# A list scheduler reckons later landings for its transfers, and the order is searched anew under them

## The chip, the cores and the metric

The kernel runs on one core of one Trainium2 chip. The metric is the device time of one launch in microseconds (us), as the median of several runs. The core has TensorE (PE in the profile) for matrix products, VectorE (DVE), ScalarE (ACT), GpSimd (POOL) and SyncE (SP). SP and POOL start transfers (DMAs) between device memory and the on-chip memory here. Each engine works through its own instructions in the order in which they were issued; between engines, semaphores make one wait for another.

## The reference

Two layers (`DEPTH = 2`) act on `x` of 512 tokens and 1024 channels. Both branches of a layer start from one projection of the normalised input.

```python
def hybrid_layer(...):
    h = rmsnorm(x, norm_g)
    proj = h @ w_in
    aq, ak, av, az, bqk, bv, bi, bf, bo, bz, ga, gb = jnp.split(proj, idx, axis=-1)
    ...
    oa = diff_attention(q, k, v, lam)                  # 8 heads: two softmax maps each, subtracted
    oa = rmsnorm(oa, attn_norm_g) * (1.0 - lam_init) * silu(az)
    ya = oa @ w_out_a
    qk = jax.nn.silu(causal_conv(bqk, conv_w, conv_b))
    hb = mlstm_chunkwise(mq, mk, mv, i_pre, f_pre)     # 8 heads: num / max(|den|, exp(-m))
    hb = sigmoid(bo) * rmsnorm(hb, mlstm_norm_g) * silu(bz)
    yb = hb @ w_out_b
    u = sigmoid(ga) * ya + sigmoid(gb) * yb
    return x + u @ w_o
```

All of it is float32.

## The kernel before

**Precision and pieces.** A float32 operand is split into a high part, rounded to the format float32r that PE multiplies, and a low part, the rest. A product then takes three matmuls: high by high, high by low, low by high. The names end in h and l: `hh`, `hl` for the normalised input, `wh`, `wl` for weights. Weights come in pieces of 128x1024 (512 KB). The projections are named as in the reference (`az`, `bqk`, `bo`, `bz`, `ga`, `gb`), `woa` and `wob` are the two output projections of the branches, `wo` the last one. A piece is the slice of weights for 128 output channels: `bo6` is the seventh of `bo`, and `wr92`, `wh92`, `wl92` are the raw, high and low tiles of the 93rd piece in the order of work. The products `bv` and `wo` are computed by a scheme of seven products (`P1` to `P7`) from sums of weight pieces (`wws`, `wwt`) and sums of inputs.

**How a piece becomes ready.** Normally `load` has SP transfer the piece into `wr`, of which there are two buffers, and `prep` has ACT cast it to `wh` and DVE subtract to get `wl`. For the names in `TUNE["dlo"]`, `dload` goes another way: POOL transfers the piece to `dh`, ACT writes its rounded negative to `dl`, and POOL transfers the piece a second time with an addition into `dl`. So `dl` is the low part without DVE or a buffer of `wr`. The sums for the seven products are made by adding transfers of POOL as well, where DVE doesn't make them.

**Heads.** Each of the eight mLSTM heads loads its decay terms in four transfers (`dd`, SP), makes scores with PE (`ms`, from `mq`, `mql` and `mk`), multiplies them with `dd`, splits them (`sdh`, `sdl`) and then sums for numerator (`num`) and denominator (`den`). `den` is a product with a matrix of ones; `msp_a` and `msp_b` are such sums for the norms of the two branches. The summand is either split over 128 rows into two parts (`hi_lo`: `msh`, `msl`, two matmuls of 128x512), or, for the heads in `foldA`, `foldM` and `foldD`, its two halves of 64 rows are added first, and the high and low parts of the sum share one tile `fo` (`fold`, one matmul):

```python
b = t2(f"fb_{name}")[L]
yield b
hl = t2(f"fo_{name}", F32R)
V.tensor_tensor(a[L], a[L], b, ALU.add)
A.copy(hl[L], a[L])
V.tensor_tensor(hl[H], a[L], hl[L].bitcast(F32), ALU.subtract)
```

**What sets the order.** The program first records every operation, with its engine, its cost by a formula and the operations it depends on, in the order of the string `TUNE["order"]` (pieces) and of due times (`attn`, `ml`, `ap`, `m0`, `mp` ...), which say after how much matmul work a head's steps are recorded. `schedule` (L293 to L443) then plays a simulation of the engines: again and again it takes the engine that can start first and picks on it the ready operation with the smallest key. Keys are nominal PE time plus a number for each kind of tile, `TUNE["bias"]`. SP takes its operations in recorded order. A transfer occupies one common road for its bytes over a rate (`rate`: 360 bytes per ns for weights, 175 for `rows` and copies, 150 for adding ones), and is reckoned landed 2000 ns after the road has it (L427). POOL spends 1000 ns on issuing one. `issue` (L462 to L469) emits all operations in the order that came out, so that nearly every row of the profile has the line L469, and table loads of ACT L468. What is on the chip is thus a fixed order per engine; the simulation's times are not.

Of the kernel before, what the change touches and what calls it, by code (L numbers as in the profile page):

```python
# [35 lines left out]

TUNE = {
    "order": (
# [4 lines left out]
    ),  # L43
    "qkt": 5,
    "gct": 18,
    "gls": 0,
    "glf": 1,
    "attn": (0, 5, 5, 9, 11, 13, 16, 16, 19, 27),
    "a0": 24,
    "ap": 18,  # L50
    "a4": 9,
    "ml": (0, 9, 16, 18, 18, 32),
    "ahead": 3,
    "lc": 4,
    "slack": 3188.5,
    "margin": 0.0,
    "pemargin": 16.8,
    "wait": 431.4,
    "swpen": 141896579.9,
    "smargin": 63.5,  # L60
    "pwait": 0.0,
    "wdiff": 7238.9,
    "wsp": 4,
    "kact": (0, 1, 2),
    "qsq": (1, 3),
    "foldA": (2, 3, 5, 6, 7),
    "foldM": (0, 1, 2, 3, 4, 5),
    "foldD": (0, 1, 2, 4, 5, 7),
    "warm": 18,
    "start": 'x0 ct ng w0 x1 w1 x2 x3',  # L70
    "prods": 'P1 P5 P2 P6 P3 P7 P4',
    "acl": 6,
    "gateA": 8,
    "gateM": 6,
    "actp": (0, 2),
    "m0": 220,
    "mp": 13,
    "m4": 9,
    "slots": 24,
    "hfd": 1,  # L80
    "tset": (0, 18),
    "silu": (),
    "pmask": 0,
    "dlo": ('az0', 'bo6', 'woa4', 'wob5'),
    "dla": 7,
    "groups": (),
    "vkeep": (('av', 0), ('av', 1), ('bv', 0), ('bv', 1)),
    "qspill": {},
    "vl": {('av', 0): 50, ('av', 1): 140, ('bv', 0): 228, ('bv', 1): 272},
    "tdve": {'bv': ('T2',), 'wo': ('T1', 'T2', 'T3')},  # L90
# [32 lines left out]
class Recorder:  # L123
# [169 lines left out]
    def schedule(self):  # L293
# [44 lines left out]
        end = [0.0] * n  # L338
        dma = 0.0
# [20 lines left out]
        while len(order) < n:  # L360
# [18 lines left out]
            s, e = best  # L379
# [18 lines left out]
            i = pick[1]  # L398
# [1519 lines left out]
```

## Time and profile before

| | before |
|---|---|
| runs | 1342.16, 1343.46, 1343.55 us, median 1343.46 |
| profiled execution | 1341.84 us, of which the span is 1340.1 us |
| granted clock of TensorE | 0.999 |
| instructions in the span | PE 6152 matmuls, DVE 1906, ACT 1880, POOL 68 |
| transferred | 158.62 MB, mean 118 GB/s |

The span runs from the first to the last instruction of the profiled execution; the 1.74 us around it are launch and end. The views used below are: the first rows of the page (busy time of each engine), the table of waits (which instruction stood idle and what ended it: time in total, number, longest), the windows (a stretch's start and end, its length, the busy time and number of instructions of PE, weight loads, DVE, ACT and POOL, the granted clock, the DMA share and GB/s), the chain that ended last (start, length, what), the instructions of one tile (shortest, median and longest duration in ns, first and last start) and the transfers (KB each, median us from issue to landing). "A <- B" in a wait means that A waited for B; in an instruction's name it means output from inputs.

### The profile page before, as it was taken

The page shows a single profiled execution, that of the slowest core. Times are in us where ns is not written, and L with a number is a line of the kernel's source. Part 1 is how long each engine was busy: PE and PEld are TensorE (multiplying, and loading weights), DVE is VectorE, ACT ScalarE, POOL GpSimd, SP SyncE. Part 2 cuts the span into 40 slices and gives each one's busy share as a digit, 9 for nine tenths or more (in the row PEclk, how much of TensorE's full clock was granted, in tenths as well). Part 3 has the DMA queues.
Part 4 walks back from the last instruction along what each step waited for, and adds up shares of the span by engine and source line. Part 5 has one row for each costly group of instructions (what it writes and reads, how often), then busy time and mean ns, then how long its engine had stood idle before and what let it go on. Part 6 is the DMA issues. An engine that isn't in the chain of part 4 may idle for free.

```text
span 1340.1 us, 17612 instructions
## 1 busy us (share of the span) xinstructions
PE 1320.6 (99%) x6152; PEld 1084.7 (81%) x6152; DVE 1065.2 (79%) x1906; ACT 925.0 (69%) x1880; POOL 55.2 (4%) x68
## 2 busy tenths in 40 slices
PE   9999999999999999999999999999999999999998
PEld 7888888888788787788788888888887887878886
DVE  7899889896588878755888988889866888787476
ACT  6878789794467787743667787888935578778242
POOL 1000000000010000001100000000001000000000
PEclk9999999999999999999999999999999999999999
DMA  6222222235364444346842232232455545353555
GB/s 218 71 65 82 76 79 81 94 94 162 119 157 118 131 117 122 99 139 156 263 125 70 65 95 64 79 99 75 113 136 159 144 119 149 80 144 97 160 152 168
DMA packets 54152, 158.62 MB, mean 118 GB/s; under 512 B 6416, under 2 KB 13200, under 8 KB 54064
## 3 DMA queue, kind: packets, MB, share of 16 engines
q1 hardware_dynamic: 48304, 136.54, 33.2%
q0 software_dynamic: 5760, 20.97, 8.1%
q8 instruction: 48, 0.79, 0.2%
q14 instruction: 40, 0.33, 0.1%
HBM read 153.23 MB, written 4.26 MB: 118 GB/s over the span
## 4 chain that ended last, share of the span: by engine, by line
PE 82%; DVE 6%; ACT 5%; DMA 5%; issue 2%; SPq 0%; DVEq 0%; ACTq 0%; POOLq 0%
PE qk L469 13%; PE av L469 9%; PE az L469 7%; PE ga L469 7%; PE woa L469 7%; PE wob L469 7%; PE gb L469 6%; PE bqk L469 5%; PE bv_P L469 4%; PE wo_P L469 4%; PE bz L469 3%; PE sc L469 3%; DMA wr<-in_wp_dram 3%; PE bo L469 2%; PE num L469 1%
## 5 line engine op out<-in xcount | busy, mean ns | idle before, releaser
L469 ACT CAST wh<-wr 128x1024 fp32r<-128x1024 f32 (+1 forms) x194 | 202.0, 1045 | 130.3 <-PE woa L469 32.7
L469 DVE TENSOR_TENSOR wl<-wr,wh 128x1024 fp32r<-128x1024 f32 (+1 forms) x196 | 233.8, 1197 | 35.4 <-ACT wh L469 34.4
L469 PE MATMUL qk<-wl,hh 128*128 128x512 f32 x256 | 96.1, 399 | 0.3 <-DVE wl L469 0.3
L469 PE MATMUL qk<-wh,hh 128*128 128x512 f32 x256 | 95.1, 397 | 0.6 <-ACT hh L469 0.6
L469 PE MATMUL qk<-wh,hl 128*128 128x512 f32 x256 | 94.8, 395 | 0.1
L469 ACT ACTIVATE p<-sc,mx,rq 128x128 f32<-128x128 f32 (+3 forms) x128 | 78.8, 619 | 9.8 <-DVE mx L469 6.8
L468 ACT ACT_TABLE_LOAD x61 | 78.3, 1283 | 1.0
L469 PE MATMUL woa<-oa,wh 128*128 128x512 f32 x224 | 73.2, 391 | 0.0
L469 PE MATMUL wob<-ob,wh 128*128 128x512 f32 x224 | 70.9, 389 | 0.0
L469 PEld LDWEIGHTS qk<-wl,hh 128*128 128x128 f32 x256 | 48.1, 188 | 10.4 <-DVE wl L469 1.1
L469 ACT CAST ks<-qkt 64x256 fp32r<-64x256 f32 x128 | 47.0, 367 | 13.5 <-DVE qs L469 12.1
L469 PEld LDWEIGHTS qk<-wh,hl 128*128 128x128 f32 x256 | 48.0, 188 | 9.8 <-DVE hl L469 0.4
L469 PEld LDWEIGHTS qk<-wh,hh 128*128 128x128 f32 x256 | 47.6, 188 | 10.0 <-ACT hh L469 0.8
L469 DVE TENSOR_REDUCE mx<-sc 128x2 f32<-128x256 f32 (+1 forms) x64 | 52.4, 818 | 0.7
L469 PE MATMUL ga<-hl,wh 128*128 128x512 f32 x128 | 50.9, 398 | 0.0
L469 PE MATMUL ga<-hh,wl 128*128 128x512 f32 x128 | 50.5, 395 | 0.0
L469 PE MATMUL ga<-hh,wh 128*128 128x512 f32 x128 | 50.3, 393 | 0.0
L469 PE MATMUL bqk<-hh,wh 128*128 128x512 f32 x128 | 50.2, 392 | 0.0
L469 PE MATMUL bqk<-hh,wl 128*128 128x512 f32 x128 | 50.2, 392 | 0.0
L469 PE MATMUL gb<-hh,wh 128*128 128x512 f32 x128 | 50.0, 391 | 0.0
L469 PE MATMUL bqk<-hl,wh 128*128 128x512 f32 x128 | 50.0, 391 | 0.0
L469 PE MATMUL gb<-hl,wh 128*128 128x512 f32 x128 | 49.9, 390 | 0.0
(355 smaller groups left out, 3841.7 us busy)
## 6 DMA issues: line engine op xcount, KB each, us to landing
wr<-in_wp_dram SPq DMA_DIRECT2D x192, 512.0 KB, 3.6
wws_wo<-in_wp_dram POOLq DMA_DIRECT2D x12, 512.0 KB, 7.1
dh<-in_wp_dram POOLq DMA_DIRECT2D x8, 512.0 KB, 3.9
dl<-in_wp_dram POOLq DMA_DIRECT2D x8, 512.0 KB, 7.2
dd<-rows SPq DMA_DIRECT2D x16, 256.0 KB, 4.0
wws_bv<-in_wp_dram POOLq DMA_DIRECT2D x8, 512.0 KB, 9.3
em<-rows SPq DMA_DIRECT2D x16, 256.0 KB, 4.7
dd<-rows SPq DMA_DIRECT2D x16, 192.0 KB, 5.3
```

What stands on the lines that cost most here:

```text
L468: self.tc.keep_in_program_order(self.nc.scalar.preload_act_table_set(self.SET_NAME[o["load"]]))
L469: self.tc.keep_in_program_order(getattr(o["e"], o["fn"])(*o["a"], **o["k"]))
```

## The change

One rule of the scheduler and the table `TUNE` change. A transfer is reckoned landed 3000 ns after the road has it, and 5500 ns if POOL issues it, where both were 2000 ns:

```diff
                 dma = max(dma, go) + size / self.rate(o)
-                end[i] = max(dma, go) + 2000.0
+                end[i] = max(dma, go) + (5500.0 if e == "POOL" else 3000.0)
```

In the table, the order of the pieces, the due times, the scheduler's margins and all biases are others; a line or two of them stand here for the rest:

```diff
-        "woa2 woa0 woa3 woa1 woa4 woa5 woa6 bv.P1 bv.P5 bv.P2 bv.P3 bv.P6 bv.P7 bqk0 bv.P4 bqk1 bo1 bqk6 bz1 bo0 bz0 "
+        "woa7 woa4 woa1 ga5 woa3 woa5 bv.P1 woa0 bv.P5 bv.P2 bv.P3 bv.P6 bv.P7 bqk0 bqk1 bv.P4 bo1 bqk6 bz1 bo0 bz0 bo4 "
...
-    "ml": (0, 9, 16, 18, 18, 32),
+    "ml": (4, 7, 12, 13, 22, 37),
...
-    "qsq": (1, 3),
-    "foldA": (2, 3, 5, 6, 7),
-    "foldM": (0, 1, 2, 3, 4, 5),
-    "foldD": (0, 1, 2, 4, 5, 7),
+    "qsq": (3,),
+    "foldA": (1, 2, 3, 4, 5, 7),
+    "foldM": (0, 1, 2, 3, 4, 5, 6, 7),
+    "foldD": (0, 1, 2, 3, 4, 5, 6, 7),
...
-    "acl": 6,
+    "acl": 7,
-    "actp": (0, 2),
+    "actp": (0, 1, 2, 3),
...
-    "dlo": ('az0', 'bo6', 'woa4', 'wob5'),
-    "dla": 7,
+    "dlo": ('az0', 'az6', 'bo1', 'bo4', 'bo6', 'bo7', 'bqk3', 'bz3', 'bz4', 'ga3', 'gb5', 'woa4', 'wob1', 'wob5'),
+    "dla": 5,
```

`dla` says how many pieces ahead `dload` looks, `acl` how many pieces ahead the sums are begun, `actp` for which token tiles ACT and not DVE scales the second softmax map, `qsq` for which token tiles ACT also sums the squares of q and k, which DVE does for the others. Of the 14 names in `dlo`, 13 are taken in each layer (for `az6` there is no room). The programs differ by this count: matmuls 6152 to 6142, transfers of POOL for `dh` and `dl` 8 to 26 each, transfers of SP 18 fewer, all of them `wr`. Both layers have the same order in themselves.

The order moves most instructions. Three places of layer 0 show how.

The first is SP's queue at the decay terms `dd` and `em` of heads 5 to 7 and the weight loads `wr87` to `wr90`. Before:

```order
L469 DMA wr87_996<-in_wp_dram 128x1024
L469 DMA wr88_1002<-in_wp_dram 128x1024
L469 DMA em0_5_980<-rows_107 128x512
L469 DMA dd0_7_1033<-rows_107 128x512
L469 DMA dd0_7_1033<-rows_107 128x384
L469 DMA dd0_7_1033<-rows_107 128x256
L469 DMA dd0_7_1033<-rows_107 128x128
L469 DMA wr89_1023<-in_wp_dram 128x1024
L469 DMA em0_6_1007<-rows_107 128x512
L469 DMA wr90_1029<-in_wp_dram 128x1024
```

And of the change, the same place:

```order
L469 DMA wr87_996<-in_wp_dram 128x1024
L469 DMA wr88_1002<-in_wp_dram 128x1024
L469 DMA em0_5_956<-rows_107 128x512
L469 DMA dd0_6_961<-rows_107 128x512
L469 DMA dd0_6_961<-rows_107 128x384
L469 DMA dd0_6_961<-rows_107 128x256
L469 DMA dd0_6_961<-rows_107 128x128
L469 DMA wr89_1008<-in_wp_dram 128x1024
L469 DMA em0_6_987<-rows_107 128x512
L469 DMA dd0_7_992<-rows_107 128x512
```

The load `wr89` stood behind the terms of head 7; it now stands behind those of head 6 and ahead of those of head 7. On ACT, its cast stood 8 rows behind that of `wr87`, whose buffer it takes over; now 26 rows.

The second is ACT around that cast and the denominator of head 6 (`dd0_6`, `msh_d0_6`, `fo_d0_6`). Before:

```order
L469 CAST fo_b0_5_992<-ms_b0_5_990 64x512
L469 ACTIVATE tbz0_6_1001<-bz0_6_999 128x512
L469 CAST wh88_1003<-wr88_1002 128x1024
L469 CAST wh89_1024<-wr89_1023 128x1024
L468 ACT_TABLE_LOAD
L469 ACTIVATE ms_b0_5_990<-ms_b0_5_990 128x512
L469 CAST msh_d0_6_1014<-dd0_6_1006 128x512
L469 ACTIVATE ms_b0_5_990<-ms_b0_5_990 128x512
```

And of the change:

```order
L469 CAST wh89_1009<-wr89_1008 128x1024
L469 COPY fb_d0_6_1014<-dd0_6_961 64x512
L469 ACTIVATE dd0_7_992<-dd0_7_992,gcol0_298 128x128
L469 ACTIVATE dd0_7_992<-dd0_7_992,gcol0_298 128x256
L468 ACT_TABLE_LOAD
L469 ACTIVATE ms_b0_5_984<-ms_b0_5_984 128x512
L469 CAST fo_d0_6_1015<-dd0_6_961 64x512
L469 ACTIVATE ms_b0_5_984<-ms_b0_5_984 128x512
```

The two weight casts no longer stand one right behind the other ahead of the table load; `wh88` now stands five rows ahead of `wh89`. Head 6 is folded, and its `fb_d` and `fo_d` take the place of `msh_d`. On PE the two matmuls for `den0_6` stood among those of `bz0_7`; the one that is left stands within the products of `num0_6`. The four `mq` casts of the fourth tile (`mq0_3`) stood in one group right behind `fb_d0_5`; two of them now stand ahead of it.

The third is POOL from the last sums of `bv` on. Before:

```order
L469 DMA wws0_bv_0_701<-in_wp_dram 128x1024
L469 DMA wws0_bv_1_706<-in_wp_dram 128x1024
L469 MEMSET mql00_0_779 64x1024
L469 MEMSET mql10_0_780 64x1024
L469 DMA dh81_887<-in_wp_dram 128x1024
L469 DMA dl81_888<-in_wp_dram 128x1024
L469 MEMSET mql00_1_931 64x1024
L469 MEMSET mql10_1_932 64x1024
```

And of the change:

```order
L469 DMA wws0_bv_0_696<-in_wp_dram 128x1024
L469 DMA wws0_bv_1_701<-in_wp_dram 128x1024
L469 DMA dh67_772<-in_wp_dram 128x1024
L469 MEMSET mql00_0_780 64x1024
L469 MEMSET mql10_0_781 64x1024
L469 DMA dl67_773<-in_wp_dram 128x1024
L469 DMA dh72_805<-in_wp_dram 128x1024
L469 DMA dl72_806<-in_wp_dram 128x1024
L469 DMA dh76_842<-in_wp_dram 128x1024
L469 DMA dl76_843<-in_wp_dram 128x1024
```

Where one pair `dh`, `dl` stood between the sums and the second set of memsets (`bo6`, piece 81), there now stands a row of pairs for pieces 67 (`bo1`), 72, 76 and more. At the start of the program, the first `dh` stood ahead of two memsets of `kl` on POOL and now stands behind them.

More of the change, by code (lines that the diff above doesn't have):

```diff
@@ L38 @@
     "order": (
[4 rows of a table removed]
[4 rows of a table added]
     ),
     "qkt": 5,
-    "gct": 18,
-    "gls": 0,
+    "gct": 17,
+    "gls": 1,
     "glf": 1,
-    "attn": (0, 5, 5, 9, 11, 13, 16, 16, 19, 27),
+    "attn": (0, 4, 6, 10, 10, 13, 14, 16, 19, 26),
     "a0": 24,
     "ap": 18,
-    "a4": 9,
-    "ml": (0, 9, 16, 18, 18, 32),
+    "a4": 18,
+    "ml": (4, 7, 12, 13, 22, 37),
     "ahead": 3,
     "lc": 4,
-    "slack": 3188.5,
+    "slack": 1705.4,
     "margin": 0.0,
-    "pemargin": 16.8,
-    "wait": 431.4,
+    "pemargin": 59.5,
+    "wait": 229.8,
     "swpen": 141896579.9,
-    "smargin": 63.5,
-    "pwait": 0.0,
-    "wdiff": 7238.9,
+    "smargin": 257.6,
+    "pwait": 3.4,
+    "wdiff": 6482.4,
     "wsp": 4,
     "kact": (0, 1, 2),
-    "qsq": (1, 3),
-    "foldA": (2, 3, 5, 6, 7),
-    "foldM": (0, 1, 2, 3, 4, 5),
-    "foldD": (0, 1, 2, 4, 5, 7),
+    "qsq": (3,),
+    "foldA": (1, 2, 3, 4, 5, 7),
+    "foldM": (0, 1, 2, 3, 4, 5, 6, 7),
+    "foldD": (0, 1, 2, 3, 4, 5, 6, 7),
     "warm": 18,
@@ L71 @@
     "prods": 'P1 P5 P2 P6 P3 P7 P4',
-    "acl": 6,
-    "gateA": 8,
-    "gateM": 6,
-    "actp": (0, 2),
-    "m0": 220,
-    "mp": 13,
+    "acl": 7,
+    "gateA": 6,
+    "gateM": 3,
+    "actp": (0, 1, 2, 3),
+    "m0": 224,
+    "mp": 16,
     "m4": 9,
     "slots": 24,
-    "hfd": 1,
+    "hfd": 0,
     "tset": (0, 18),
@@ L88 @@
     "qspill": {},
-    "vl": {('av', 0): 50, ('av', 1): 140, ('bv', 0): 228, ('bv', 1): 272},
+    "vl": {('av', 0): 48, ('av', 1): 142, ('bv', 0): 216, ('bv', 1): 254},
     "tdve": {'bv': ('T2',), 'wo': ('T1', 'T2', 'T3')},
-    "bias": {'wo': -3700.0, 'woh': -4650.0, 'p5_wo': -40630.0, 'ws1_wo': -2200.0, 'ws0_wo': -900.0, 'wt1_wo': 1400.0, 'qk1_0x': 2050.0, 'qk1_2x': -800.0, 'qk0_0x': -1600.0, 'wt0_wo': -2500.0, 'sgb': -62610.0, 'hh': 46060.0, 'mx': -20530.0, 'uhZ': -27170.0, 'mk': 43610.0, 'junk': -5820.0, 's1_bv': -39750.0, 'gf': 31320.0, 'num': -33940.0, 'wwt0_wo': -19430.0, 'msh_d': -58100.0, 'p5_bv': -37800.0, 'rows': 12370.0, 'xn': -8470.0, 'gm': 8760.0, 'uz': 32170.0, 'posf': -43160.0, 'rn': 19970.0, 'kl': -9190.0, 'hl': 16820.0, 'dq': -31380.0, 'mq': -15890.0, 'ht': 5190.0, 'ulA': 33830.0, 'gi': -18610.0, 'fo_a': -11000.0, 'fb_d': -29470.0, 'ms': 11600.0, 'fb_a': 46170.0, 'x1d': -13700.0, 'wws0_bv': 13690.0, 'uhY': 52620.0, 'ones': -38970.0, 'epsc': 38080.0, 'fo_d': 610.0, 'msl_a': 18670.0, 'ld': -23490.0, 'qkt': 9270.0, 'wl': -1080.0, 'av': -5090.0, 'sinv': -13980.0, 'em': -31530.0, 'posi': -26850.0, 'wo1_P': 18850.0, 'msp_b': -26610.0, 's1_wo': 8300.0, 'lhS': 44090.0, 'qt': -9580.0, 'par': -27350.0, 'x': -47250.0, 'qk': 14220.0, 'gc': -1800.0, 'yc_bv': 18990.0, 'gt': -7890.0, 'xr': -21880.0, 'uhA': 910.0, 'den': 16400.0, 'uy': 4190.0, 'ua': 27800.0, 'wws1_wo': 11070.0, 'msh_b': -2210.0, 'sdl': -23400.0, 'gct': 23610.0, 'bv1_P': -14030.0, 'sc': 1320.0, 'ulB': 2690.0, 'gw': -6490.0, 'lfA': 21040.0, 'rot': -6840.0, 'rnh': -18750.0, 'p': 11640.0, 'wr': 7810.0, 'sdh': 26790.0, 'ms_a': -2120.0, 'wob': 6220.0, 'ga': -5620.0, 'oa': -4640.0, 'taz': 14610.0, 'cv': -2050.0, 'mql': -4100.0, 'woa': -10920.0, 'sbo': -7780.0, 'qss': 26460.0, 'eps': 38460.0, 'ob': 23330.0, 'sq': 41410.0, 'wws0_wo': -10600.0, 'zeroc': 460.0, 'bqk': -8560.0, 'msp_a': -3170.0, 'ss': 15870.0, 'saz': 3230.0, 'glf': -990.0, 'uhB': -10180.0, 'sums': -10050.0, 'msl_d': 11670.0, 'dl': -8260.0, 'ctab': 7630.0, 'ml': 1230.0, 'ng': 7810.0, 'bz': 32150.0, 'wws1_bv': 15060.0, 'wwt1_bv': -28210.0, 'dd': 9260.0, 'lq': 21360.0, 'msh_a': -5670.0, 'wwt0_bv': -2330.0, 'tbz': 9290.0, 'ct': -6870.0, 'ut': 13230.0, 'stab': -9760.0, 'uh': -5810.0, 'ulZ': 3610.0, 'qs': -4160.0, 'fb_b': -6210.0, 'ms_b': 750.0, 'az': -4050.0, 'gft': -12820.0, 'pb': 1950.0, 'cosv': 580.0, 'fo_b': -2780.0, 'zw': 6490.0, 'qy': -190.0, 'rq': -2550.0, 'sbz': 2390.0, 'wh': 12500.0, 'dh': 4160.0, 'warm': -7690.0, 'llS': 2270.0, 'wo0_P': -750.0, 'ks': -6730.0, 'bo': -2000.0, 'ul': -40.0, 'msl_b': 80.0, 'wwt1_wo': 130.0, 'bv0_P': -1420.0, 'lneps': 2440.0, 'bv': -300.0, 'ang': 20.0, 'gb': -2700.0},
@@ L92 @@
-    "drain": 76.2,
-    "group": 4190.8,
+    "bias": {'wo': -3700.0, 'woh': -4650.0, 'p5_wo': -39580.0, 'ws1_wo': -2200.0, 'ws0_wo': -900.0, 'wt1_wo': 1400.0, 'qk1_0x': 2050.0, 'qk1_2x': -800.0, 'qk0_0x': -1600.0, 'wt0_wo': -2500.0, 'sgb': -66930.0, 'hh': 27580.0, 'mx': -18960.0, 'hl': 89830.0, 'ht': 64040.0, 'sums': -6160.0, 'wl': 103390.0, 'qt': -8720.0, 'av': -6550.0, 'ua': -17580.0, 'rows': 145480.0, 'ctab': -11600.0, 'gm': 31160.0, 'junk': 590.0, 's1_wo': -66970.0, 'bv1_P': -41090.0, 'zw': -86700.0, 'bv0_P': -40730.0, 'ss': 14830.0, 'msl_d': 2120.0, 'msh_d': -8700.0, 'rq': 1700.0, 'mql': -38680.0, 'bqk': -8230.0, 'ulZ': 57710.0, 'wws0_wo': -26210.0, 'dl': 660.0, 'ang': 9470.0, 'qs': -8850.0, 'wh': 4830.0, 'sdl': -36480.0, 'dq': -19930.0, 'az': -5860.0, 'fo_a': 36250.0, 'msh_a': -10420.0, 'fb_b': -20280.0, 'sq': -4760.0, 'gft': 13730.0, 'oa': -4740.0, 'gc': -10830.0, 'bo': 19840.0, 'msl_b': -15940.0, 'msh_b': -9480.0, 'ms_b': 26330.0, 'kl': 5440.0, 'mk': 10100.0, 'rn': -9280.0, 'lq': 1670.0, 'stab': 25950.0, 'ut': 33970.0, 'par': -9200.0, 'uhY': 25220.0, 'msp_b': 3170.0, 'mq': 32790.0, 'xn': -13680.0, 'wws1_wo': -22920.0, 'ob': -22130.0, 'dd': 10410.0, 'gcol': 23900.0, 'ml': 12130.0, 'wwt1_wo': -6780.0, 'dh': -11690.0, 'sc': 37850.0, 'llS': 9360.0, 'ulB': 20440.0, 'xr': -25650.0, 'rot': 12480.0, 'ones': 5490.0, 'gi': -2220.0, 'wo1_P': 34470.0, 'warm': -26240.0, 'lneps': -57660.0, 'glf': 9810.0, 'wo0_P': -2880.0, 'fo_b': -23040.0, 'epsc': 5380.0, 'eps': 2610.0, 's1_bv': 4950.0, 'gf': -920.0, 'ct': 580.0, 'gt': 25320.0, 'wwt0_bv': 14510.0, 'wwt0_wo': 19830.0, 'qk': 9230.0, 'taz': 35990.0, 'msp_a': 7970.0, 'woa': -1430.0, 'ulA': -21920.0, 'ms': 40650.0, 'fb_d': 9040.0, 'gw': -2260.0, 'qss': -5700.0, 'sbz': -6860.0, 'posi': -18500.0, 'p5_bv': -10460.0, 'ul': -3650.0, 'num': 820.0, 'uh': 9760.0, 'saz': -630.0, 'lfA': -4660.0, 'ks': 23600.0, 'gct': -17270.0, 'fb_a': 18590.0, 'sbo': -1030.0, 'sdh': -6190.0, 'uy': 380.0, 'x1d': -10710.0, 'uhZ': -5850.0, 'ga': -11870.0, 'wws1_bv': -10710.0, 'pb': 10340.0, 'zeroc': 5310.0, 'cosv': -3050.0, 'tbz': -1890.0, 'posf': -510.0, 'rnh': -4920.0, 'p': -2930.0, 'qkt': 3010.0, 'ms_a': 2920.0, 'uhA': 2980.0, 'msl_a': -3500.0, 'qy': 12160.0, 'uz': 4730.0, 'gb': -3170.0, 'em': -15410.0, 'ld': -1290.0, 'ng': -680.0, 'wwt1_bv': 19550.0, 'uhB': -990.0, 'den': 6770.0, 'ulY': -6430.0, 'wws0_bv': 3320.0, 'yc_bv': 19760.0, 'out_0_dram': -11770.0, 'wr': 3520.0, 'bz': -170.0, 'bv': -4890.0, 'cv': 260.0, 'x': 70.0, 'fo_d': -540.0, 'lhS': 690.0},
@@ L94 @@
+    "drain": 26.1,
+    "group": 2441.2,
     "lates": ('bv',),
-    "risk": 192.1,
-    "late": 333.7,
+    "risk": 113.4,
+    "late": 420.1,
 }
```

6 rows, old and new, of the table TUNE are left out of this document.

## The prediction

> **What bounds the kernel now.** I read the page's first rows, the table of waits of TensorE (PE), the windows, and then the chain that ended last around each long wait.
>
> ```profile
> PE 1320.6 (99%) x6152; PEld 1084.7 (81%) x6152; DVE 1065.2 (79%) x1906; ACT 925.0 (69%) x1880; POOL 55.2 (4%) x68
> 316.19 28.81 PE woa L469 x127
> 20.00:310.00 290.00, 290.00 (x1419) 240.00 (x1418) 256.21 (x588) 238.03 (x630) 6.56 (x8) 1.00 0.28 84
> 385.00:545.00 160.00, 155.59 (x716) 127.84 (x714) 130.32 (x185) 118.61 (x169) 3.87 (x5) 1.00 0.46 123
> ```
>
> PE is busy for 1320.6 of the 1340.1 us of the span, at a clock of 1.00. Two things can therefore be won: matmuls that are no longer issued, and the 19.5 us in which PE stands idle. What a matmul costs is read from an undisturbed stretch of the chain: 127 of them in 28.81 us are 0.227 us each. (The durations near 0.39 us in other rows overlap.) The windows say where the idle time lies. From 20 to 310 us, attention, PE doesn't stop at all. From 385 to 545 us, the mLSTM heads of layer 0, it stands for 4.4 us, and in the same stage of layer 1 for about as long. The table of waits says what ended the larger ones (time in total, how often, longest):
>
> ```profile
> PE den L469 <- ACT msh_d L469: 4.3, 2, 2.4
> PE ms L469 <- ACT mq L469: 2.5, 2, 1.5
> PE bv_P L469 <- DVE s_bv L469: 1.6, 2, 0.8
> PE den L469 <- DVE fo_d L469: 1.1, 2, 0.7
> PE bv_P L469 <- DVE yc_bv L469: 0.7, 1, 0.7
> ```
>
> These five rows are 10.2 us, over half of the idle time, and all lie in the sums of bv and the mLSTM heads. What hides behind "ACT msh_d" is seen in the chain, at the wait of head 6 of layer 0:
>
> ```profile
> 535.30 6.21 DMA wr<-in_wp_dram
> ...
> 541.60 0.07 ACT wh L469
> 541.66 1.00 issue
> 542.66 1.28 ACT L468
> 543.96 0.63 ACT ms_b L469
> 544.59 0.52 ACT msh_d L469
> 545.10 0.04 issue
> 545.15 0.50 PE den L469
> ```
>
> ScalarE (ACT) stands in order at the cast of a weight piece. The piece took 6.21 us to land, and the denominator's own cast was queued behind it: cast, table load, ms_b, msh_d, and PE stood for up to 2.4 us. So the bound is PE's work, plus a handful of places where an in-order ACT waits for a landing that the planner had put earlier. The old planner adds 2.0 us to 512 KB at 360 B/ns (1.46 us), 3.46 us in all. The trace has:
>
> ```profile
> wr<-in_wp_dram SPq DMA_DIRECT2D x192, 512.0 KB, 3.6
> dh<-in_wp_dram POOLq DMA_DIRECT2D x8, 512.0 KB, 3.9
> dl<-in_wp_dram POOLq DMA_DIRECT2D x8, 512.0 KB, 7.2
> DMA to landing us min/median/max: 5.6/7.2/9.3
> DMA to landing us min/median/max: 2.5/3.6/10.0
> ACT wh L469 <- DMA wr<-in_wp_dram: 32.4, 19, 3.0
> ```
>
> The fourth row is that of dl, the fifth that of wr. A typical load is reckoned about right; the slow ones, up to 10.0 us, are not, and 19 casts waited 32.4 us for one. The new figures are 1.46 + 3.0 = 4.46 us for a load, and for an adding transfer 1.0 + 3.5 + 5.5 = 10.0 us instead of 6.5, above the slowest that the trace shows (9.3).
>
> **The change, part by part**, against the profiled execution of 1341.84 us (span 1340.1). The median of the runs, 1343.46, lies 1.62 above it; the same difference is applied to it.
>
> *Fewer matmuls.* The folds take one ones-matmul in place of two: foldA has one head more, foldM two and foldD two, in each of two layers, so 10 matmuls of 128x512 go. 10 x 0.227 = **-2.3 us**. PE is the bound, so this comes through whole. Each costs ACT and VectorE (DVE) instead, an extra copy and adds of 64 rows.
>
> ```profile
> L469 ACT COPY fb_d<-dd x12: 618/619/622, 405.0 to 1218.6; 64x512 f32<-64x512 f32 x12
> L469 DVE TENSOR_TENSOR dd<-dd,fb_d x12: 673/676/685, 406.0 to 1219.2; 64x512 f32<-64x512 f32 x12
> L469 DVE TENSOR_TENSOR wl<-wr,wh x196: 679/1218/1228, 10.1 to 1318.2; 128x1024 fp32r<-128x1024 f32 x188, 128x512 fp32r<-128x512 f32 x8
> L469 ACT ACTIVATE dl<-dh x8: 1046/1052/1061, 17.1 to 1231.2; 128x1024 fp32r<-128x1024 f32 x8
> ```
>
> That is 1.3 us more per folded head in the chain ahead of its denominator, on engines that are busy for 130 and 119 of the 160 us of that stage. I cost it at nothing, because den is placed among matmuls that don't need it (bz's in the old order, num's in the new), which PE does meanwhile; uncovered it would be at most 10 x 1.3 = 13 us, and I keep a little of that below.
>
> *Eighteen more lo parts by transfers.* Of 14 names, 13 are taken in each layer (4 before), so 18 pieces change. DVE loses 18 x 1.218 = 21.9 us of wl; ACT's negation at 1.052 us takes the place of a cast of 1.05 us. Both lie behind PE (79% and 69% busy), so the gain is relief and not time. 18 pieces are read twice: 9.4 MB on 158.6. In the window from 385 us, six of them add 3.1 MB to 123 GB/s x 160 us = 19.7 MB; the DMA share would go from 0.46 to about 0.53. The lo part has to be there by its first matmul: the order puts the adding transfer ahead of that by some 10.2 us (gb5), 11.6 (bo1), 12.0 (bqk3) and 13.9 us (bo7) of PE's matmuls at 0.227 us each, the others 16 us and more. dl's slowest landing, 9.3, fits them all, by 0.9 us in the tightest. Nothing is booked; rival 2 has the price.
>
> *Later landings, new order.* This moves loads on SP's queue, adding transfers on GpSimd's (POOL's), and casts on ACT. Wait by wait:
> - den, 4.3 us: wr89's load is issued one group of four dd loads earlier on SP, and on ACT its cast stands 26 rows behind that of wr87, whose buffer it takes over, where it stood 8; head 6 is folded, so the msh_d cast and a second den matmul are gone. **-3.5**: what replaces it, fo_d, is itself late in one case of two (1.1 us). Bounds: 0 and -4.3.
> - ms for mq, 2.5 us:
>
> ```profile
> 526.56 0.62 ACT fb_d L469
> ```
>
> The four mq casts of the fourth tile no longer stand in a row behind fb_d; two come ahead of it, and fb_d's 0.62 us and a cast or two are the longest wait of 1.5 us. **-1.3**, half; bounds 0 and -2.5.
> - bv_P for s_bv, 1.6 us, and for yc_bv, 0.7 us:
>
> ```profile
> 367.55 7.43 DMA wwt_bv<-in_wp_dram
> ...
> 377.99 0.61 DVE yc_bv L469
> 378.73 3.45 PE bv_P L469 x14
> ```
>
> The second ends a chain that starts in an adding transfer of 7.43 us. The order now issues that one about 12 us earlier, and P4's pieces get a bqk piece ahead. **-1.2 and -0.5**; bounds 0 and -2.3 together.
> - den for fo_d, 1.1 us. The wait came from the landing of dd:
>
> ```profile
> 445.13 6.53 DMA dd<-rows
> 451.75 0.43 DVE dd L469
> 452.21 0.70 DVE fo_d L469
> ```
>
> rows is reckoned 1 us later as well, against 6.53. **-0.4**; bounds 0 and -1.1.
> - The rest of the idle time (start, the sums of wo): no term, since I read no move there that frees or binds PE.
> - The first POOL row, dh9, now stands behind two memsets of kl, 1.94 us, so 0.5 MB less competes with the first loads, which run at 395 GB/s from 4 to 6 us:
>
> ```profile
> 1.99 1.94 POOL L469 MEMSET kl<- 64x1024 f32 x2
> 4.00:6.00 2.00, 2.00 (x6) 1.56 (x5) 0.00 (x0) 1.56 (x4) 0.00 (x0) 1.00 1.11 395
> ```
>
> 512 KB at that rate are 1.3 us, of which I take **-0.5**; bounds 0 and -1.3.
> - Waits at new places. An order with no wait exists for a whole stage (20 to 310 us), so 0 is one end. The other is that the waits tied to landings return elsewhere: 4.3 + 1.6 + 0.7 = 6.6 us. The landing of 6.21 lies 1.75 us above the new 4.46, where it lay 2.75 above 3.46, so about two thirds of the gap stays open; but few of the 19 late casts reached PE. I take a third, **+2.2**, which also covers the folds' longer chains.
>
> Sum: -2.3 - 3.5 - 1.3 - 1.2 - 0.5 - 0.4 - 0.5 + 2.2 = **-7.5 us**, 1343.46 to **1336.0**. All bounds at their good end: -2.3 - 4.3 - 2.5 - 2.3 - 1.1 - 1.3 = -13.8 (1329.7). With every wait kept and the 6.6 added anew, +4.3 (1347.8).
>
> A rule against my price for the adding transfers: the trace has 3.9 us for a plain 512 KB from POOL and 7.2 for an adding one. The Trainium skill, "DMA: Bandwidth & Descriptors", "Anatomy of one DMA — SWDGE (gpsimd) path", fits 2.0 us + bytes/436e3, by which I estimate 3.2 us for either. By it the new reckoning would be needlessly late and rival 2 could not occur; the measured 7.2 decides, and the sum stays.
>
> **The rivals.**
> 1. *Only PE's work goes.* The waits move but stay as long: the planner's constants can't foretell a single landing of 10.0 us, and the casts that waited are 19, not the two I looked at. -2.3 us: 1341.2, a result within 0.2%. Against it: two of the waits have a queue order behind them that is gone.
> 2. *Slower: adding transfers land after their first use.* Where a dl lands later than the lead above, PE stops, since nothing of that product can be issued past it. It decides from 10.2 us on. For it: sums for bv, the same kind of transfer under more traffic, reach further than dl:
>
> ```profile
> DMA to landing us min/median/max: 7.9/9.3/11.7
> ```
>
> (the row is wws_bv's). Four times as many pairs follow each other on POOL's queue. With landings of 13 us, gb5, bo1 and bqk3 are late by 2.8 + 1.4 + 1.0 = 5.2 us a layer, 10.4 in all; after -7.5 that is 1346.4, and without the gain at the waits 1351.6. Against it: median 7.2, and four leads only.
> 3. *Nearly all waits of the table that rest on a landing go*, and relief of DVE lets chains end early: the good end above with no new wait, 1329.7 to 1331.
> 4. *Traffic.* Share 0.46 to 0.53 lengthens each wr landing by the same 16%; waits tied to landings grow from 6.6 to 7.7 instead of going: -2.3 + 1.1 = -1.2, 1342.3. For it: from 4 to 6 us the share is 1.11 and wr's slowest landing is 10.0. Against: 84 and 123 GB/s are far from 395. The Trainium skill, "Trainium Kernel Development and Optimization", "Key Constraints", says that transfers issued by SP, ACT and POOL run on the same 16 DMA engines and interleave, which speaks for this rival: moving lo parts to POOL opens no second road.
>
> **How the numbers follow.** About 0.2% (2.7 us) is what a measurement of this kernel tells from no change: 1340.8 to 1346.1. Forecast 0.58 (0.56 faster, 0.02 same); rival 1 0.15 (0.06 faster, 0.09 same); rival 2 0.08 (0.03 same, 0.05 slower); rival 3 0.14 (faster); rival 4 with its neighbours 0.05 (0.02 same, 0.03 slower, where more than landings grow). Together 0.76 faster, 0.16 same, 0.08 slower. The range goes from rival 3's end, 1329.5, past rivals 1 and 4 to 1344.0; it leaves out rival 2 and the upper bounds, some 0.12.
>
> **What would show it.** PE has 6142 matmuls, and the windows of attention still no idle time. In the waits of PE "den <- ACT msh_d" is gone, "ms <- ACT mq" about halved, and the rows of den, ms and bv_P sum to under 4 us, from 10.2. ACT's wait for wr falls from 32.4 us. Wrong: PE rows "<- DMA dl", or dl's slowest landing above 10.2 (rival 2); the same sum under other names (rival 1); wr's median well above 3.6 (rival 4).

## The result and the profile after

The changed kernel takes 1323.77 us (median of four runs, 1322.92 to 1324.30), the one before 1343.51 (1342.16 to 1343.56). The ratio is 0.9855, with a 95% interval of 0.9838 to 0.9872: 19.7 us less, where 7.5 were forecast, and below the forecast's range. The profiled execution's span went from 1340.1 to 1322.4 us, 17.7 less.

The page's first row and the table of PE's waits (time in total, how often, longest) of the changed kernel:

```profile
PE 1311.3 (99%) x6142; PEld 1086.2 (82%) x6142; DVE 1046.0 (79%) x1874; ACT 936.8 (71%) x1803; POOL 80.7 (6%) x104
PE num L469 <- DVE ms_b L469: 3.0, 2, 1.5
PE qk L469 <- ACT hh L469: 2.0, 1, 2.0
PE warm L469 <- DVE ml L469: 1.6, 1, 1.6
PE ht L469 <- DVE junk L469: 0.3, 1, 0.3
```

The four rows are the whole table. All five rows shown of before are gone, those of wo_P too; one large new row, num for ms_b, has come, and at the start the row of qk for hh has grown from 0.6 us to 2.0. PE's idle time is 11.1 us where it was 19.5. The stage of the heads in layer 0, same columns as before:

```profile
385.00:545.00 160.00, 158.53 (x740) 131.99 (x739) 131.63 (x190) 126.15 (x182) 11.85 (x16) 1.00 0.56 142
```

In the same 160 us PE now does 740 matmuls, where it did 716 (not quite the same ones, since the order is another). The DMA share rose from 0.46 to 0.56. The transfers (KB each, median us to landing), then shortest, median and longest landing of dl and of dh, and ACT's wait for weight loads:

```profile
wr<-in_wp_dram SPq DMA_DIRECT2D x174, 512.0 KB, 3.7
dh<-in_wp_dram POOLq DMA_DIRECT2D x26, 512.0 KB, 6.1
dl<-in_wp_dram POOLq DMA_DIRECT2D x26, 512.0 KB, 6.0
DMA to landing us min/median/max: 5.2/6.0/9.8
DMA to landing us min/median/max: 3.8/6.1/9.4
ACT wh L469 <- DMA wr<-in_wp_dram: 14.0, 8, 3.3
```

No adding transfer into a dl landed later than 9.8 us, and no row of PE names a dl: rival 2 did not happen. ACT's waits for loads fell from 32.4 us (19 times) to 14.0 (8 times).

PE's "busy" time hides short gaps between matmuls. So I also added up, from the trace, the gap between the starts of neighbouring matmuls beyond the first one's own time (227 ns for 512 columns, 173, 118 and 59 for 384, 256 and 128, 109 for a transpose, the usual distances in the trace). Own times fell by 2.3 us (1287.8 to 1285.5), the gaps by 15.6. By the product whose matmul came late, gaps of 20 ns and more, in us, for the two kernels and four of the experiments below:

| late product | before | after | old rule | old list | 100 ns later | ms_b moved |
|---|---|---|---|---|---|---|
| den | 6.1 | 0.0 | 0.0 | 0.3 | 0.0 | 0.0 |
| wo_P | 4.3 | 0.6 | 2.4 | 0.6 | 0.5 | 0.6 |
| bv_P | 3.0 | 0.1 | 4.5 | 0.1 | 0.1 | 0.1 |
| ms | 3.8 | 1.1 | 2.8 | 2.9 | 1.4 | 1.3 |
| num | 2.5 | 5.2 | 2.0 | 2.9 | 2.4 | 1.7 |
| wob | 0.1 | 0.6 | 3.2 | 10.9 | 6.1 | 0.6 |
| qk | 6.5 | 8.0 | 10.0 | 7.4 | 7.6 | 8.2 |
| all gaps, small ones too | 46.6 | 31.0 | 44.3 | 49.6 | 36.5 | 27.5 |

Den, wo_P, bv_P and ms together gave 15.4 us; num and qk took back 4.2; the rest came in small amounts in many places, bo, bz, av, ga and sc with 0.6 to 0.8 each.

Own times are those at full clock, so a lowered clock shows as gaps too. The windows show two such stretches, the first at the start of the changed kernel, the second in a_dlo4 of the experiments below (the old list; the same happens there in layer 1); the granted clock is the 0.50:

```profile
12.82:16.23 3.41, 3.06 (x10) 2.09 (x9) 3.41 (x7) 3.23 (x7) 0.00 (x0) 0.50 0.82 293
570.95:577.78 6.83, 4.98 (x12) 3.88 (x13) 4.64 (x7) 5.62 (x7) 0.00 (x0) 0.50 0.00 0
```

The matmuls of the first stretch have gaps of 2.0 us; those in the same stretch of the kernel before, at a clock of 1.00, have 0.8.

### The profile page after: what moved, and what is told of

Same layout as the page of the kernel before. It is cut to its first block, busy times and chain, and to the rows that moved or that the text cites. A ratio compares the mean times of both kernels' runs of the same rounds, so it can differ in the third digit from the quotient of the medians.

```text
span 1322.4 us, 17563 instructions
## 1 busy us (share of the span) xinstructions
PE 1311.3 (99%) x6142; PEld 1086.2 (82%) x6142; DVE 1046.0 (79%) x1874; ACT 936.8 (71%) x1803; POOL 80.7 (6%) x104
## 4 chain that ended last, share of the span: by engine, by line
PE 96%; DMA 2%; ACT 1%; SPq 0%; DVE 0%; issue 0%; DVEq 0%
PE qk L469 13%; PE av L469 9%; PE az L469 7%; PE ga L469 7%; PE bqk L469 7%; PE wob L469 7%; PE gb L469 7%; PE woa L469 7%; PE bz L469 6%; PE wo_P L469 6%; PE bv_P L469 6%; PE bo L469 5%; PE sc L469 3%; PE num L469 2%; PE ms L469 2%; PE ut L469 1%
## 5 line engine op out<-in xcount | busy, mean ns | idle before, releaser
L469 ACT CAST wh<-wr 128x1024 fp32r<-128x1024 f32 (+1 forms) x176 | 183.0, 1044 | 119.6 <-PE wo_P L469 16.3
L469 DVE TENSOR_TENSOR wl<-wr,wh 128x1024 fp32r<-128x1024 f32 (+1 forms) x178 | 212.2, 1195 | 47.1 <-ACT wh L469 45.0
L469 PE MATMUL wob<-ob,wh 128*128 128x512 f32 x192 | 61.2, 391 | 0.0
L469 POOL DMA_DIRECT2D dl<-in_wp_dram x26 | 22.6, 870 | 588.2 <-ACT dl L469 489.2
L469 PE MATMUL av<-wh,hl 128*128 128x512 f32 x128 | 50.5, 395 | 0.0
L469 PE MATMUL av<-wl,hh 128*128 128x512 f32 x128 | 50.5, 394 | 0.0
L469 PE MATMUL av<-wh,hh 128*128 128x512 f32 x128 | 49.1, 392 | 0.0
L469 PEld LDWEIGHTS woa<-oa,wh 128*128 128x128 f32 x224 | 42.0, 188 | 8.4
L469 ACT CAST uh<-ut 128x128 fp32r<-128x128 f32 (+2 forms) x80 | 29.7, 371 | 24.7 <-PE ut L469 20.0
L469 PE MATMUL az<-hl,wh 128*128 128x512 f32 x112 | 44.4, 397 | 0.0
```

The lines of the kernel that those rows point to most:

```text
L469: self.tc.keep_in_program_order(getattr(o["e"], o["fn"])(*o["a"], **o["k"]))
```

## The experiments

Three theories stood against each other. Theory 1: the later landings in the planner's rule are what takes PE's waits away. Theory 2: the gain belongs to an order that was searched for one rule, one table and one list, and any step off it costs time. Theory 3: the 18 fewer wl relieve DVE, and that is the gain. All ratios are to the kernel before in the same session, with 95% intervals; the changed kernel has 0.9855.

### One part put back into the changed kernel, or the rule alone put into the old one

Old rule (a_land2), old list (a_dlo4) and old folds (a_fold) in the changed kernel; new rule in the kernel before (b_land). In each the scheduler makes a new order.

```diff
a_land2, and the other way round b_land:
-                end[i] = max(dma, go) + (5500.0 if e == "POOL" else 3000.0)
+                end[i] = max(dma, go) + 2000.0
a_dlo4:
+    "dlo": ('az0', 'bo6', 'woa4', 'wob5'),
a_fold:
+    "foldA": (2, 3, 5, 6, 7),
+    "foldM": (0, 1, 2, 3, 4, 5),
+    "foldD": (0, 1, 2, 4, 5, 7),
```

> The changed kernel with the old rule (every transfer reckoned landed 2000 ns after the road has it), the new table kept. Theory 1, that the later landings are what keeps PE's waits away: the old kernel's sort of waits returns, 10.2 us in den, ms and bv_P and some 4 in wo_P, so 1330 to 1337 us. Theory 2, that a table fits only the rule it was searched under and any departure costs: also slower, but with waits at any place and not behind landings, 1330 to 1340. Theory 3, that DVE's relief by 18 fewer wl carries the gain: 1324 to 1326, since the relief stays.

> The kernel before with the new rule and its old table. Theory 1: most of the waits of 10.2 us behind landings go, 1334 to 1339 us. Theory 2: the old table doesn't fit the new rule, 1343 to 1355. Theory 3: no relief, so no gain, 1342 to 1345.

> The changed kernel with the old four names in dlo: 18 pieces are loaded once and split by ACT and DVE again, 18 x 1.218 = 21.9 us more of DVE. Theory 1: within 3 us of the changed kernel, 1322 to 1327. Theory 2: 1330 to 1340, as for any other departure. Theory 3: most of the gain goes, 1335 to 1343.

> The changed kernel with the old foldA, foldM and foldD: ten matmuls of 128x512 more. Theories 1 and 3: 10 x 0.227 = 2.3 us more, 1325 to 1328. Theory 2: 1330 to 1340.

Measured: a_land2 1337.57 us, ratio 0.9943 (0.9928 to 0.9958); b_land 1356.33, 1.0080 (1.0049 to 1.0111); a_dlo4 1341.75, 0.9978 (0.9965 to 0.9991); a_fold 1328.45, 0.9873 (0.9844 to 0.9902). ACT's wait for loads in b_land and in a_land2:

```profile
ACT wh L469 <- DMA wr<-in_wp_dram: 10.4, 8, 3.1
ACT wh L469 <- DMA wr<-in_wp_dram: 20.1, 11, 4.2
```

In these two pairs ACT's waits go the way of the rule: with the old table they fall from 32.4 to 10.4 us, and with the new one they rise from 14.0 to 20.1 when the rule goes. But the row is not the rule's alone: with the new rule kept it is 23.2 us in a_fold, 24.0 in a_near2 and 24.1 in b_all (both below). And b_land is 0.8% slower than before. Its waits of PE stand elsewhere, the first two of its table being

```profile
PE az L469 <- ACT wh L469: 3.7, 2, 1.8
PE bv_P L469 <- ACT wh L469: 2.2, 2, 1.1
```

and at az ACT's cast stands behind casts of qs and ks, with no landing in the chain. So theory 1 falls in the form that I gave it: in b_land the rule shortens ACT's waits and den's (gaps of den 1.0 us instead of 6.1), not those of bv_P (6.4 instead of 3.0), and more is lost elsewhere. Nor does den need the rule: its gaps are 0.0 in a_land2 and in b_dlo (below), which have the old one. Theory 3 gained from a_dlo4, which gave back nearly everything. But most of that is one place, after the last head (chain: start, length, what):

```profile
563.70 4.54 PE wob L469 x19
568.24 0.25 PE msp_b L469
...
572.13 0.62 ACT ob L469
...
572.80 1.22 PE wob L469 x2
```

Between msp_b and wob six steps of DVE and ACT, ob the last, follow each other with gaps of some 0.02 us. Nothing stands in their way, but in PE's order no other matmul is placed ahead of that wob. The wait costs about 4 us in each layer, and the stretch at half clock, which begins within it, another 2.5: some 12.7 of the 18.9 us by which the span grew. a_fold lost 4.7 us by medians and 2.4 by the ratios, about the ten matmuls that theories 1 and 3 allow for.

### Small steps off the rule

```diff
a_near:
+                end[i] = max(dma, go) + (5600.0 if e == "POOL" else 3100.0)
a_near2:
+                end[i] = max(dma, go) + (5400.0 if e == "POOL" else 2900.0)
b_near:
+                end[i] = max(dma, go) + 2100.0
```

> The changed kernel with landings reckoned 100 ns later still, 3100 and 5600 ns. The rule says the same of the chip; only the fit of table and rule is disturbed. Theory 1: 1322 to 1327 us. Theory 2: 1330 to 1340, about as much as the step back to 2000 ns (1337.6).

> The changed kernel with landings reckoned 100 ns earlier, 2900 and 5400 ns, the other side of the run with 100 ns more (+5.8 us). Joint theory: 1326 to 1334 us, with waits at one or two new places. If the rule's value itself mattered and the last step was chance: 1322 to 1325.

> The kernel before with every landing reckoned 100 ns later, 2100 ns. It tells how far an old table falls off its rule with a step that says nothing of the chip: theory 2 expects 2 to 10 us more, 1346 to 1354; theory 1 within 3 us of 1344.

Measured: a_near 1329.54 us, 0.9887 (0.9868 to 0.9905); a_near2 1330.15, 0.9887 (0.9871 to 0.9903); b_near 1342.56, 0.9985 (0.9974 to 0.9995). 100 ns to either side cost the changed kernel some 0.3%, 4 us or more (the spans grew by 5.4 and 7.2), at the low end of what theory 2 asked for or below it. So a run of the planner loses this much without any reason in the chip, and of the losses above only those of a_land2 (13.2 us of span) and a_dlo4 are clearly larger; that of a_fold (4.2) is not. In a_near a new place waits, wob for ob (3.5 us in the waits); in a_near2 num for ms_b grows from 3.0 to 4.2. Behind these waits the granted clock fell to 0.5 for 3.4 us, once in a_near and in each layer of a_near2; 1.7 and 3.1 us of their gaps lie there. The kernel before lost nothing by its one step, against theory 2; perhaps its table was not fitted to its rule that closely.

### DVE's work taken away or given back, in an unchanged order

Here the engines' order stays as it was. a_dve adds a block of twelve small memsets on DVE behind the negation of each of the 18 new dl; a_dve2 adds such blocks in the stage of gb and wob, ten in each layer, so 20 and not the 18 that I had expected; b_fastwl replaces each wl of the kernel before by a copy and one column, and so leaves the low parts of the weights out.

```diff
a_dve, in issue():
+            if o["eng"] == "ACT" and o["a"][0].tensor.name in self.pad:
+                for _ in range(12):
+                    self.tc.keep_in_program_order(self.nc.vector.memset(self.scratch, 0.0))
a_dve2: the same behind ua <- sgb, ua and the first uy of each layer
b_fastwl, in issue():
+            if o["eng"] == "DVE" and o["kind"] == "wl":
+                y, p, q, op = o["a"]
+                self.tc.keep_in_program_order(self.nc.vector.tensor_copy(y, q))
+                self.tc.keep_in_program_order(self.nc.vector.tensor_tensor(y[:, :1], p[:, :1], q[:, :1], op))
+                continue
```

> The changed kernel in its own order on every engine, with 18 idle blocks of twelve small memsets on DVE, one behind each negation of the 18 new dl: about as much DVE work as the 18 wl that the change took away. Theory 3, that DVE's relief is the gain: most of the loss of the run with the old four names (18 us) comes back, 1334 to 1342 us. Theory 2, that the loss came from an order that was not searched for that table: 1323 to 1326, as DVE stands idle for a fifth of the span.

> The changed kernel in its own order with the same 18 blocks of twelve memsets on DVE (12 x 112 ns = 1.34 us each), but all in the stage of gb and wob, where DVE is busy for 27.8 of 57 us. If DVE's total is what counts, the time rises as in the first run of these blocks, by 15 to 21 us. If only DVE work inside the heads' chain of scores counts, the time rises by less than 3 us.

> The kernel before in its own order; each wl is a copy of wh and one column of the subtraction, so the low parts of the weights are left out of the result. The dependencies stay, DVE's work per piece falls from 1.22 to some 0.6 to 1.0 us, in all 196 pieces. If DVE's load sets the waits of the kernel before, 5 us or more are gained, 1330 to 1339. If its waits hang on landings and on ACT's order, less than 3 us, 1341 to 1345.

Measured: a_dve 1344.70 us, 0.9998 (0.9988 to 1.0007); a_dve2 1336.62, 0.9934 (0.9908 to 0.9959); b_fastwl 1341.89, 0.9973 (0.9962 to 0.9984). The blocks, and the rows of a_dve's waits that are new or larger:

```profile
L472 DVE MEMSET scratch<- x216: 112/112/112, 194.3 to 1254.3; 128x64 f32 x108
PE ms L469 <- DVE dd L469: 9.2, 6, 1.6
PE num L469 <- DVE ms_b L469: 3.4, 2, 1.7
PE ms L469 <- ACT mq L469: 2.4, 2, 1.2
PE qk L469 <- ACT wh L469: 2.1, 2, 1.1
PE msp_b L469 <- DVE fo_b L469: 1.8, 2, 0.9
```

The first block in the order of time (start, length, what):

```profile
194.30 2.22 DVE L472 MEMSET scratch<- 128x64 f32 x12
```

The memsets are busy for 112 ns each, 24.2 us in all, but start 192 ns apart, so that a block holds DVE for 2.22 us and the 18 blocks for 40.0. That is nearly twice the 21.9 us of the 18 wl, more than I had expected them to stand for. The span rose from 1322.4 to 1342.6, by 20.2: half of what was put in came through to PE, although DVE stands idle for a fifth of the span. In the stage of gb and wob, where DVE is busy for half the time, 20 blocks, 44.4 us, still cost 11.1 us (span 1333.5). Of these, 4.3 us are gaps behind PE's waits at wo, where the granted clock was 0.5 for 3.4 and 6.8 us, and 6.1 are the waits themselves, one row:

```profile
PE wo_P L469 <- DVE wl L469: 6.1, 2, 3.0
```

I had expected under 3 us there; the blocks stand ahead of the wl of the sums for wo, which begin right behind. The kernel before gained 0.3% by cheaper wl (its page has DVE at 990.8 us instead of 1065.2), and its largest waits stayed:

```profile
PE den L474 <- ACT msh_d L474: 4.6, 2, 2.5
PE ms L474 <- ACT mq L474: 1.8, 2, 1.1
```

So DVE's load is not what held the old order. In the new one, DVE can't take blocks of this length at the places tried without PE waiting; what 18 wl at their old length would cost there is not measured.

### List, table and all other parts alone

b_dlo is the kernel before with only the longer list (13 names, az6 among them in place of wob1, which the changed kernel takes); a_tab has the new table but the old rule, list, dla and folds; b_all has the new rule, list and folds on the old table.

```diff
b_dlo and b_all (b_all with the new rule and folds besides):
+    "dlo": ('az0', 'az6', 'bo1', 'bo4', 'bo6', 'bo7', 'bqk3', 'bz3', 'bz4', 'ga3', 'gb5', 'woa4', 'wob5'),
a_tab (with the old dlo, dla and folds besides):
+                end[i] = max(dma, go) + 2000.0
```

> The kernel before, old rule and old table, with only the longer list of names in dlo (13 of the 14; 26 pairs of dh and dl). Theory 3, that DVE's relief carries the gain: 1326 to 1336 us. Theory 2, that an order holds only for the table it was searched for: 1340 to 1355, with waits at new places.

> The changed kernel's table (order of pieces, due times, margins, biases) alone: old rule, old names in dlo and old folds. If the table carries the gain by itself: 1322 to 1332 us. If it holds only together with the rule and the list it was searched with: 1338 to 1352.

> The kernel before with the new rule, the longer list in dlo (13 names) and the new folds, on its old table. If these parts carry the gain: 1322 to 1334 us. If they need the table that was searched with them: 1340 to 1358.

Measured: b_dlo 1345.54 us, 0.9998 (0.9985 to 1.0011); a_tab 1360.05, 1.0102 (1.0082 to 1.0121); b_all 1350.98, 1.0045 (1.0030 to 1.0059). In a_tab the wait of den for msh_d is back, and more:

```profile
PE ms L469 <- DVE dd L469: 8.4, 6, 2.7
PE den L469 <- ACT msh_d L469: 4.3, 2, 2.2
ACT wh L469 <- DMA wr<-in_wp_dram: 40.3, 16, 4.7
```

The table alone is 1.0% slower, everything but the table 0.45% slower, and both together 1.45% faster. None of the parts holds the gain by itself; it is in the order that came out of all of them. (In the profiled executions of b_land, a_tab and b_all, stretches at half clock hold 3.5, 6.7 and 3.4 us of the gaps, so part of what they lose is the clock's.)

### Single moves in a fixed order

b_cast takes the kernel before and moves one weight cast in each layer behind the table load, ms_b and msh_d of head 6. a_num takes the changed kernel and moves the table load and two ms_b of head 1 ahead of the dd activations of head 3.

```diff
b_cast (ACT):
-CAST wh89
 ACT_TABLE_LOAD
 ACTIVATE ms_b0_5
 CAST msh_d0_6
 ACTIVATE ms_b0_5
+CAST wh89
a_num (ACT):
+ACT_TABLE_LOAD
+ACTIVATE ms_b0_1 x2
 ACTIVATE dd0_3 (four)
-ACT_TABLE_LOAD
-ACTIVATE ms_b0_1 x2
```

> The kernel before, in its own order, with one cast moved in each layer: the weight cast that stood in ACT's stream ahead of the table load, ms_b and msh_d of head 6 stands behind them. If the late landing behind that cast is what PE waits for at den, the row den for ACT msh_d (4.3 us) goes and the time falls by 3.5 to 4.5 us. If the wait only moves on to the next link of the chain, the time falls by less than 1.5 us.

> The changed kernel in its own order, with one group moved in each layer: the table load and the two ms_b activations of head 1 stand ahead of the four dd activations of head 3, which wait for their transfers, and no longer behind them. If PE's wait for ms_b (3.0 us) comes from the landing of dd (8.16 us in the chain) by ACT's order alone, it goes: 2 to 3.5 us less than the changed kernel. If DVE's own place in the chain holds it, no change.

Measured: b_cast 1337.49 us, 0.9952 (0.9937 to 0.9967), span 1335.6 instead of 1340.1; a_num 1321.13, 0.9827 (0.9805 to 0.9848), span 1318.8 instead of 1322.4. In b_cast the row den for msh_d is gone, and the gaps fell by 4.4 us, den's alone from 6.1 to 1.7. This confirms cause and price as the waits of before gave them: a late landing behind one cast, 4.4 us, removed by moving that cast. The chain that a_num was made for, in the changed kernel:

```profile
439.02 8.16 DMA dd<-rows
...
447.27 0.44 DVE dd L469
...
447.73 0.80 ACT dd L469 x2
...
448.55 1.28 ACT L468
...
449.85 0.64 ACT ms_b L469
...
451.17 0.76 DVE ms_b L469
...
452.07 0.88 PE num L469 x3
```

It is the same pattern on another tile: ACT stands at a piece of dd that landed after 8.16 us, and ms_b, the last reader of the accumulator that the next num needs, is queued behind. With the move the row is gone and num's gaps fell from 5.2 to 1.7 us.

a_best adds two moves at the start: hh's cast ahead of the first weight cast, and the first dh issued only after the first wl.

```diff
ACT:
+CAST hh0
 CAST wh0
-CAST hh0
DVE:
 TENSOR_TENSOR wl0
+MEMSET dh9 128x64 (the first dh transfer waits for it)
```

> The changed kernel in its own order with the move of ms_b at head 1, and two at the start: hh's first cast stands ahead of the first weight cast on ACT, and the first dh is issued only after the first wl (by a memset of 64 of its columns on DVE). The trace of the changed kernel has 2.0 us of wait for hh there, and wr landing 0.4 us later than before the change: 0.5 to 1.8 us less than with the move of ms_b alone, 1319.3 to 1320.6 us; no change if the first wl is what PE needs last.

Measured: 1320.42 us, 0.9818 (0.9804 to 0.9831), span 1317.9. The start gave 0.9 us of span against a_num, less than the intervals separate, and a_num's execution had 3.4 us at a clock of 0.5 there, which this one had not. What is left in its table:

```profile
PE warm L502 <- DVE ml L502: 1.6, 1, 1.6
PE qk L502 <- ACT wh L502: 1.2, 1, 1.2
PE qk L502 <- DVE wl L502: 0.5, 2, 0.3
```

These are waits at the start alone. This version has the lowest time here.

## Why the prediction was wrong

- **Fewer matmuls, -2.3:** right. 6142 matmuls; at 0.227 us each the ten that are gone are the 2.3 us, and a_fold, which has them back, lost no less.
- **den, -3.5 and -0.4:** the mechanism was right, shown by b_cast; the size was not. The gaps went whole, 6.1 us, as they do in most of the orders tried, under the old rule too. I held back a part for a late fo_d, and none was late.
- **ms, -1.3, and bv_P, -1.2 and -0.5:** measured -2.7 and -3.0. Taking half of a wait where the order shows only that it gets shorter was the mistake. Bv_P's gain hangs on the new rule with the new table: with the old rule it is 4.5 us.
- **"The rest of the idle time (start, the sums of wo): no term":** this step failed outright. wo_P's gaps fell from 4.3 to 0.6 us. They are 0.5 to 0.7 with the old list, the old folds or a rule off by 100 ns, 2.4 with the old rule, and 4.8 or more in every run on the old table whose order is made anew. So they went with the new table and, for a part, the rule. I had not weighed that place, whose rows of before are:

```profile
PE wo_P L469 <- DVE wl L469: 0.9, 3, 0.3
PE wo_P L469 <- DVE xn L469: 0.8, 1, 0.8
PE wo_P L469 <- DVE xr L469: 0.8, 1, 0.8
```

  Two of the three wait for the additions that read wo's results (xn in layer 0, xr in layer 1), not for a landing, and with the gaps right behind them they are 2.1 of the 4.3 us. Which move of the new order removed them is not shown, since none was tried alone.
- **Start, -0.5:** not gained. With dh9 behind the memsets it is issued at 2.64 us, beside the first weight load; ng landed 1.1 us earlier, but the first weight cast began at 9.39 us and not at 9.02. qk's gaps rose by 1.5 us, those of warm, ht and qk together by 1.0. But 1.2 us of difference lie in the stretch at half clock, so the sign is not shown.
- **Waits at new places, +2.2:** right in kind, but twice as large. num's gaps rose by 2.7 us by a landing of dd of 8.16 us, late even against the new rule; az, qkt and wob added 2 more.
- **"Eighteen more lo parts: nothing is booked, relief and not time":** true of the old order (b_dlo no change, b_fastwl 0.3%) and not safe in the new one. The cover that I named, PE's 99% against DVE's 79%, is an average: in a_dve, blocks that hold DVE for 40.0 us in the new order cost 20.2 us. That the search turned the relief into time is likely by this and by a_dlo4, but not shown.
- **Rivals.** Rival 1, only PE's work goes, fell with the gaps. Rival 2 fell: no landing of dl above 9.8 us. Rival 4 asked for longer landings: wr's median moved from 3.6 to 3.7 us, dh's from 3.9 to 6.1, without a wait of PE behind it. (Two readings were loose: the pairs on POOL's queue are 26 in place of 8, a little over three times as many and not four, and in the heads of layer 1 PE stood for 3.4 us, not for about the 4.4 of layer 0.) Rival 3 was the right kind, nearly all waits gone, and its end of 1329.7 was still short, as it counted only the rows that I had quoted. The Trainium skill, "Trainium Kernel Development and Optimization", "Key Constraints", has the transfers from SP, ACT and POOL run on the same 16 engines and interleave. The rise of dh from 3.9 to 6.1 us agrees with it, and the price did not reach PE.

Of the miss of 12.2 us by medians, 10.2 show in the spans (17.7 against 7.5). Of those, den, ms and bv_P account for 4.8 (11.7 in place of 6.9) and wo_P for 3.8; the start (+1.0 with warm and ht, instead of -0.5) and the new waits (4.7 instead of 2.2) take back 4.0; the remaining 5.6 are many gaps of under a microsecond, for which no single move was tried. That rule, list and table hold the gain only together is what a_land2, a_dlo4, a_tab and b_all show, each of them for the one order that the planner made of it; only den and num have their cause shown by a single move. Why a search under this rule ended at an order so much better is not shown: no search was made under another.

## What to carry to other kernels

In an order that a planner made, price each wait by its chain and expect it to go whole if the row that holds it moves; look at every place with a wait, also at those where no edit is seen. Don't call an engine covered by its share of busy time: put known work into the fixed order and see what comes through, and measure how long it really holds the engine. Parts of a searched change can't be judged one by one, since each run of the planner makes another order; a single move in a fixed order can.

## What was not expected of the hardware

- The plain 512 KB transfers of POOL took 6.1 us in the median where 26 were issued, 3.9 where 8 were; the adding ones took 6.0 instead of 7.2.
- In or behind some waits of PE the granted clock fell to 0.5 for 3.4 or 6.8 us: in a_dlo4 6.8 us in each layer at a wait of 3.9 us, where 12 matmuls took 4.98 us and not 0.227 each, in a_near2 3.4 us at waits of up to 2.3. Not at all of them: den's 2.4 us in the kernel before has no such stretch. The table of waits doesn't show this price, the gaps and the windows do.
- The memsets of 128x64 on DVE in a_dve are busy for 112 ns each and start 192 ns apart.
- While a head's dd and em come from one row spread over 128 partitions, the DMA engines are busy and move little. The changed kernel's DMA view from 434 to 449 us, in 40 slices (busy tenths, then GB/s):

```profile
DMA  4969799998986999879796788983511158999999
GB/s 76 229 120 273 240 371 262 382 360 295 306 284 246 311 290 273 208 138 63 102 112 83 76 61 68 78 25 15 16 12 23 42 187 324 359 273 208 208 186 240
```

From some 440.8 to 443.8 us (slices 19 to 26) they are 60 to 90% busy at 61 to 112 GB/s; in slices 10 to 16 they moved 246 to 311 at much the same share. The dd that num waited for was under way then. Its packets are of 2 KB and less, those of the weights of 4 KB; whether that or the one row does it is not shown.
